# One square a chunk, later sums, far tiles between near ones, later scan masks: four moves in a hybrid encoder step

## The chip, the cores and the metric

The kernel runs on one core of one Trainium2 chip. The metric is the device time of one execution in microseconds: the median of several runs. A second source is one profiled execution, from which the views of the profile (timelines, waits, stretches of the span) come.

## The reference

One layer of a streaming encoder is computed for two groups of tokens that share the weights: 256 tokens of a prompt and 32 of a running stream, 288 columns in all. The model width is 2048.

```python
xn   = rmsnorm(x, norm_mix_pre)
proj = xn @ w_in            # u_pool (1024) | z (2048) | xBC (2560) | dt (32)
pool = pool_mixer(u_pool)   # trailing means over windows 2, 4, 8, 16
y    = ssd_scan(conv_silu(xBC), dt, A, B, C, D, h0)    # 32 heads, state 128
ssd  = grouped_rmsnorm(y * silu(z))
x    = x + rmsnorm(concat(pool, ssd) @ w_out, norm_mix_post)
h    = rmsnorm(x, norm_ffn_pre)
up   = causal_dwconv(h @ w_up, width=3)                # 2 * 5632 columns
x    = x + rmsnorm((silu(gate) * value) @ w_down, norm_ffn_post)
```

The outputs are x for both groups and the new histories and states of the pooling, the convolutions and the scan. All inputs and outputs are 32-bit floats.

## The kernel before

**Tiles and products.** Activations lie transposed: 16 tiles of 128 features by 288 tokens. Every large product is made from three matmuls in a faster 32-bit format: each weight is split into a high part (`whi`, a copy on ACT, L152) and a low part (`wlo`, raw weight less high part, on DVE, L153), each activation too (`xn`, `hn` and others), and `mm3` (L166) adds high by high, high by low and low by high. So for each block of weights (1024 elements a partition) a DMA from SP brings the raw block, ACT splits it, DVE makes the low part, and PE runs 24 matmuls of 288 columns on it. The high parts and the low parts have a fixed number of buffers each, so a split can begin only when PE is done with an older one.

**Order.** A scheduler orders the instructions of each engine by priorities and by a model of their times. Each engine takes its queue strictly in that order, so an instruction that waits holds all behind it. Three things bind the scheduler: `pin` (also `keep_in_program_order`) keeps the written order among pinned instructions, `issue_after` puts one instruction behind another, and `high_priority` draws a part ahead.

**The start (L353 to L397).** The first 768 columns of the input projection are worked off in 11 chunks of the 16 feature tiles (`CHUNKS`; chunks 6 to 10 hold two tiles each). `prepare(i)` makes chunk i's operands one chunk ahead of the products: `xn` high on ACT (L318), the weight's high part on ACT (L330), `xn` low (L321) and the weight's low part (L334) on DVE. Beside it run the squares of the input for the first norm: `squares(q)` squares two tiles on ACT (L353) into `sq`, which has one buffer, and adds them to `sq2` on DVE (L354). The table `SQUARES` says in which chunk's preparation which squares stand. In chunk 9, after 24 products, two matmuls `prs` (L391) sum the squares over the features; ACT takes the root (L394) and DVE the reciprocal (L395), `rstd`, by which every result of the projection is scaled later. The products of a chunk run on PE at L397.

**The scan's masks.** The projection goes on in groups of columns: groups of `xs` (input of the scan, after a convolution with tanh, L459), then groups of `z`. For each quad of heads `ssd_first` fetches the decays and makes `ce` (an exponential, L617), `ssd_tokens` fetches the tokens, and `ssd_masks` makes the mask `m`: 12 Relus (L653), an exponential (L656) and a product on DVE (L658). `run_masks` calls it; `XS_RATE` and `Z_RATE` say after which group how many quads are made. `ssd_products` (L678 to L684) uses the masks on PE.

**Between mixer and FFN (L1097 to L1127).** `x1[s]`, the 16 result tiles of the output projection (tiles `mg`), are each multiplied by the second norm's factor `rm` on DVE (L1119). Then the layer's input is added: for the near tiles (s below `NEAR`, 8) it lies in SBUF and DVE adds it (L1121); for the far tiles GpSimd starts a DMA that adds it from HBM (L1123, 144 KB). `hn_of(t)` then makes the FFN's operand: `hn` high on ACT (L1100), low on DVE (L1101), the square on ACT (L1108, `sq` with two buffers), and the sum of squares on DVE (L1115). The matmuls of the up projection that read `hn` and the weight splits of that projection run at the same time on PE, ACT and DVE.

Of the kernel before, what the change touches and what calls it, by code (L numbers as in the profile page):

```python
# [1 line left out]

# [8 lines left out]
AF = mybir.ActivationFunctionType  # L11
# [17 lines left out]
KD = D_MODEL // P  # L29
# [7 lines left out]
MW = 416  # L37
EVAC = 100
SUMS_AFTER = 2
XS_RATE = (0, 0, 1, 0, 1, 0, 0, 1)  # L40
Z_RATE = (1, 0, 1, 1, 1, 1, 0, 0)
PAIR_XS = (7,)
PAIR_Z = (1, 4, 6)
# [2 lines left out]
CHUNKS = ((0, 1), (1, 1), (2, 1), (3, 1), (4, 1), (5, 1), (6, 2), (8, 2), (10, 2), (12, 2), (14, 2))  # L46
# [8 lines left out]
TURN_AT = 13  # L55
FC_GAP = 48
NEAR = 8
W_GAP = 48
W_ROOM = 64
TURNED_FIRST = (4, 5)  # L60
# [9 lines left out]
def body(  # L70
# [23 lines left out]
    act, dve, pool, pe, sp = nc.scalar, nc.vector, nc.gpsimd, nc.tensor, nc.sync  # L94
# [210 lines left out]
    def prepare(i):  # L305
# [4 lines left out]
        w_ = xin.tile([P, 2 * n * NB + W_ROOM], F32R, tag="w", bufs=3, name="w")  # L310
        hi, lo = (w_[:, c : c + n * NB].rearrange("p (k c) -> p k c", k=n) for c in (0, n * NB + W_GAP))
        w = (hi, lo)
# [34 lines left out]
    def squares(q):  # L347

        src = xg[:, KD + 2 * NT * q : KD + 2 * NT * (q + 1)]
        if q == 0:  # L350
            return pin(act.activation(sq2, src, AF.Square))
        o = xin.tile([P, 2 * NT], F32, tag="sq", bufs=1, name="sq")
        pin(act.activation(o, src, AF.Square))  # L353
        pin(dve.tensor_tensor(sq2, sq2, o, op=ALU.add))  # L354

    SQUARES = {4: (0,), 5: (1,), 6: (2,), 7: (3, 4), 8: (5,), 9: (6,), 10: (7,)}
    early = ExitStack()
    early.enter_context(tc.high_priority(offset=2000))
    ahead_w = [prepare(0)]
    for i, (kb, n) in enumerate(CHUNKS):  # L360
        if i + 1 < len(CHUNKS):
            ahead_w.append(prepare(i + 1))
            for q in SQUARES.get(i + 1, ()):
                squares(q)
        if i == 5:
            first_load(10)
            pin(act.activation(ones_r, ones, AF.Copy))
            pin(dve.memset(ebuf[0][:, 0:1], 0.0))
            for e in ebuf + ubuf:
                pin(pool.memset(e, 0.0))  # L370
        if i == 6:
            pin(dve.tensor_tensor(
                w_dt, w_dt, g_mix_pre.unsqueeze(2).broadcast_to([P, KD, HEADS]), op=ALU.mult
            ))
        if i == len(CHUNKS) - 2:
            pin(dve.tensor_tensor(sq2[:, :NT], sq2[:, :NT], sq2[:, NT:], op=ALU.add))
            sq_r = xin.tile([P, 2 * NT], F32R, tag="sq", bufs=1, name="sq_r")
            pin(dve.tensor_copy(sq_r[:, :NT], sq2[:, :NT]))
            pin(dve.tensor_tensor(sq_r[:, NT:], sq2[:, :NT], sq_r[:, :NT].bitcast(F32), op=ALU.subtract))
        w = ahead_w.pop(0)  # L380
        products = [
            (r, m, k, x) for m in (2, 3, 4, 5, 0, 1) for k in range(n)
            for r, x in (((0, 0), (1, 0), (0, 1)) if i in TURNED_FIRST else ((0, 0), (0, 1), (1, 0)))
        ]
        if i == 0:
            products.sort(key=lambda q: ((q[1] + 4) % 6 // 2, q[0], q[3]))
        for q, (r, m, k, x) in enumerate(products):
            if i == len(CHUNKS) - 2 and q == 24:
                p_ = aux([P, NT], "prs")
                for c in (slice(0, NT), slice(NT, 2 * NT)):  # L390
                    pin(pe.matmul(p_, ones_r, sq_r[:, c], start=c.start == 0, stop=c.start > 0))  # L391
                rstd = const.tile([P, NT], F32, tag="spread", bufs=3, name="rstd")
                last_split[:] = [
                    pin(act.activation(rstd, p_, AF.Sqrt, bias=eps_t, scale=1.0 / D_MODEL)),  # L394
                    pin(dve.reciprocal(rstd, rstd)),  # L395
                ]
            pin(pe.matmul(  # L397
                first[m], w[r][:, k, m * P : (m + 1) * P], xn[kb + k][:, x, :],
                start=kb + k + r + x == 0, stop=kb + k == KD - 1 and r == 1,
            ))  # L400

    for k in range(KD):
        c = slice(HEADS * (k % 4), HEADS * (k % 4 + 1))
# [33 lines left out]
    def conv_in(i, p_):  # L437
# [6 lines left out]
        pool.tensor_copy(e[:, 259:262], hist_c[:, :, i])  # L444
        return e

    def conv_out(i, e, out):

        pool.tensor_copy(
            sc_stage[:, :, :, i], e[:, 256:326].rearrange("p (s c) -> p s c", c=35)[:, :, 0:3]  # L450
        )
        c = mp.tile([P, 291], F32, tag="conv", bufs=2, name="conv")
        act.activation(c, e[:, 0:291], AF.Identity, bias=cb_[:, i : i + 1], scale=cw[:, 0, i : i + 1])
        for r in range(1, 4):
            dve.scalar_tensor_tensor(
                c, e[:, r : r + 291], cw[:, r, i : i + 1], c, op0=ALU.mult, op1=ALU.add
            )
        th = mp.tile([P, 291], F32, tag="tanh", bufs=2, name="tanh")
        act.activation(th, c, AF.Tanh)  # L459
        dve.scalar_tensor_tensor(out[:, :NP_], th[:, :NP_], 1.0, c[:, :NP_], op0=ALU.add, op1=ALU.mult)  # L460
        dve.scalar_tensor_tensor(out[:, NP_:], th[:, 259:], 1.0, c[:, 259:], op0=ALU.add, op1=ALU.mult)

# [35 lines left out]
    with tc.high_priority(offset=EVAC):  # L498
        for i, v in enumerate(v4):
            c = slice(HEADS * i, HEADS * (i + 1))  # L500
# [109 lines left out]
    def ssd_first(q):  # L610

        gb = mp.tile([P, 4, MW], F32, tag="gb", bufs=2, name="gb")
        pool.dma_start(out=gb, in_=g_d[4 * q : 4 * q + 4, :].unsqueeze(0).broadcast_to([P, 4, MW]))
        h0t = mp.tile([P, 2, P], F32, tag="h0t", bufs=2, name="h0t")
        sp.dma_start(out=h0t.rearrange("p i c -> p (i c)"), in_=state_nq[:, 2 * P * q : 2 * P * (q + 1)])
        ce = mp.tile([P, 4, NS], F32, tag="ce", bufs=2, name="ce")
        act.activation(ce, gb[:, :, 384:], AF.Exp)  # L617
        cs = bc[2 + q // 4][:, NP_:]
        dve.tensor_tensor(ce, ce, cs.unsqueeze(1).broadcast_to([P, 4, NS]), op=ALU.mult)
        ready.append((gb, h0t, ce))  # L620
# [3 lines left out]
    exps = []  # L624
# [7 lines left out]
    def ssd_masks(q):  # L632


        gi = q // 4
        if not q:
            ssd_first(0)
        gb, h0t, ce = ready[q]
        xw = tokens.pop(q)
        w = tok[:, :, 1, 4 * q : 4 * q + 4].unsqueeze(3).broadcast_to([P, 3, 4, 64])  # L640
        o = xw.rearrange("p b (r q) -> p b r q", r=4)
        with ExitStack() as order:
            if masked:
                order.enter_context(tc.issue_after(masked[-1].ins))
            dve.tensor_tensor(o, o, w, op=ALU.mult)
        m = mp.tile([P, 4, MW], F32, tag="m", bufs=2, name="m")
        for j in range(4):
            for b, (lo_, hi_) in enumerate(((0, 256), (256, 384), (384, MW))):
                h = 4 * q + j
                with ExitStack() as order:  # L650
                    if exps:
                        order.enter_context(tc.issue_after(exps[-1].ins))
                    act.activation(  # L653
                        m[:, j, lo_:hi_], gb[:, j, lo_:hi_], AF.Relu, bias=tok[:, b, 0, h : h + 1], scale=-1.0
                    )
        exps.append(act.activation(m, m, AF.Exp, scale=-1.0))  # L656
        masked.append(
            dve.tensor_tensor(m, m, cbt[:, gi : gi + 1, :].broadcast_to([P, 4, MW]), op=ALU.mult)  # L658
        )

        if q % 2 == 0:
            ssd_first(q + 1)
        return xw, m, h0t, ce
# [155 lines left out]
    for i in range(1, NX // 2):  # L819
        if XS_RATE[i]:  # L820
            ssd_tokens(quads[0])
# [3 lines left out]
        if i in PAIR_XS:  # L825
            run_pair()
        run_masks(XS_RATE[i])
    for i in range(NX // 2):
# [90 lines left out]

    xT = op_.tile([P, NEAR, NT], F32, name="xT2")  # L920
    x1 = []
# [45 lines left out]
    for gi in range(2):  # L967
        c = slice(gi * P, (gi + 1) * P)
# [96 lines left out]
    for grp in ((0, 1), (2,), (3,), (4,), (5,), (6, 7)):  # L1065
# [13 lines left out]
        if grp[0] == 0:  # L1079
            sp.dma_start(out=xT.rearrange("p k n -> p (k n)"), in_=x_g[:, KD : KD + NEAR * NT])  # L1080
            sp.dma_start(out=new_sconv, in_=sc_stage.rearrange("p s r t -> p (s r t)"))
# [33 lines left out]
            pin(dve.tensor_tensor(xsum, xsum, squares.pop(t - 1), op=ALU.add))  # L1115

    todo = list(range(KD))
    for s in range(KD):
        pin(dve.tensor_tensor(x1[s], x1[s], rm, op=ALU.mult))  # L1119
        if s < NEAR:  # L1120
            pin(dve.tensor_tensor(x1[s], x1[s], xT[:, s, :], op=ALU.add))  # L1121
        else:
            pin(pool.dma_start(out=x1[s], in_=x_g[:, KD + NT * s : KD + NT * (s + 1)], accum_op=ALU.add))  # L1123
        while todo and todo[0] + (1 if todo[0] < NEAR else NEAR) <= s:
            hn_of(todo.pop(0))
    while todo:
        hn_of(todo.pop(0))  # L1127
# [94 lines left out]
    for q in range(4):  # L1222
        for b in range(2):
            t = apool.tile([P, 512], F32, tag="a", name="xr")
# [94 lines left out]
    for n_, part_ in enumerate(parts):  # L1319
        for i, t in enumerate((A, B)):  # L1320
            for k, hi, lo in part_:
                c, end = slice(i * P, (i + 1) * P), k == HALF - 1
# [140 lines left out]
```

## Time and profile before

| | us |
|---|---|
| median of 3 runs | 1305.62 (1305.27 to 1305.78) |
| profiled execution, whole | 1306.34 |
| its span | 1304.6 |
| PE busy | 1296.9 (99%), 10043 instructions |
| DVE busy | 897.0 (69%) |
| ACT busy | 671.6 (51%) |
| GpSimd (POOL) busy | 251.7 (19%) |
| granted clock of PE | 1.00 of full speed |

A row of a timeline gives the start (us from the span's start), the time to the end of the last, the engine, the line, the operation, the tiles written and read, and how many of a kind stand behind one another; in brackets is the idle time before it and what ended that. A matmul's time includes its way through the array, so PE's pace is read from the distance of two starts. PEld is PE's loading of the stationary operand.

### The profile page before, as it was taken

To read this page: it belongs to the slowest core of one execution; us is meant where nothing else is said; L and a number is where in the kernel's file an instruction comes from. 1 tells how busy PE (TensorE), PEld (TensorE's weight loads), DVE (VectorE), ACT (ScalarE), POOL (GpSimd) and SP (SyncE) were. 2 spreads that over 40 slices of the span, in tenths; PEclk is the share of its full clock that TensorE was granted. 3 is DMA by queue.
4 is the path that set the end of the run, shared out by engine and by line. 5 is a ranking of instruction groups with operands and counts; after the bars stand their busy time and mean duration, and the time that the engine had idled before them with its cause. 6 is when DMAs were issued, how large, how long until landed. Compare 5 with 4: busy or idle time off the path is not lost.

```text
span 1304.6 us, 25289 instructions
## 1 busy us (share of the span) xinstructions
PE 1296.9 (99%) x10043; PEld 1286.6 (99%) x10043; DVE 897.0 (69%) x1531; ACT 671.6 (51%) x1013; POOL 251.7 (19%) x399
## 2 busy tenths in 40 slices
PE   9999999999999999999999999999999999999998
PEld 9999999999999999999999999999999999999997
DVE  7999987989655588867766744336666666664454
ACT  7557676646544567554544433334444454444442
POOL 2343231222222231211211100001111111201110
PEclk9999999999999999999999999999999999999999
DMA  8668877445767478766545455455545555466663
GB/s 329 204 211 274 250 242 232 137 166 169 242 213 229 140 198 259 210 185 202 172 162 166 160 170 175 157 175 182 174 162 166 175 175 165 163 233 191 209 182 113
DMA packets 110326, 251.75 MB, mean 193 GB/s; under 512 B 64768, under 2 KB 73888, under 8 KB 87936
## 3 DMA queue, kind: packets, MB, share of 16 engines
q1 hardware_dynamic: 103856, 233.36, 55.7%
q0 software_dynamic: 5824, 16.13, 4.3%
q8 instruction: 78, 1.28, 0.4%
q10 hardware_dynamic: 528, 0.66, 0.2%
q14 instruction: 40, 0.33, 0.1%
HBM read 237.11 MB, written 13.00 MB: 192 GB/s over the span
## 4 chain that ended last, share of the span: by engine, by line
PE 96%; DMA 1%; DVE 1%; ACT 1%; issue 0%; SPq 0%; ACTq 0%
PE acc L166 91%; PE acc_x L166 1%; DMA raw<-in_w_first 1%; PE py L678 1%; PE acc L1324 0%; DVE w L334 0%; PE acc L1325 0%; DMA xg<-in_x_g 0%; PE acc_t L1347 0%; DVE sq L354 0%; PE py L680 0%; PE acc_x L397 0%; PE acc L397 0%; DVE xn L321 0%; PE pst L1036 0%
## 5 line engine op out<-in xcount | busy, mean ns | idle before, releaser
L153 DVE TENSOR_TENSOR wlo<-raw,whi 128x1024 fp32r<-128x1024 f32 (+1 forms) x396 | 472.7, 1196 | 297.1 <-ACT whi L152 296.1
L152 ACT ACTIVATE whi<-raw 128x1024 fp32r<-128x1024 f32 (+1 forms) x396 | 408.0, 1033 | 471.1 <-PE acc L166 381.3
L166 PE MATMUL acc<-hn,whi 128*128 128x288 f32 x2752 | 539.0, 294 | 0.5 <-ACT hn L1100 0.4
L166 PEld LDWEIGHTS acc<-hn,whi 128*128 128x128 f32 x2752 | 436.3, 188 | 1.5 <-ACT hn L1100 0.8
L166 PE MATMUL acc<-hn,wlo 128*128 128x288 f32 x1376 | 399.6, 291 | 0.0
L166 PEld LDWEIGHTS acc<-hn,wlo 128*128 128x128 f32 x1376 | 259.0, 188 | 0.0
L166 PE MATMUL acc<-fa,whi 128*128 128x288 f32 x1320 | 257.5, 293 | 0.0
L166 PE MATMUL acc<-xn,whi 128*128 128x288 f32 x1216 | 238.5, 294 | 0.0
L166 PEld LDWEIGHTS acc<-fa,whi 128*128 128x128 f32 x1320 | 208.9, 188 | 0.0
L166 PEld LDWEIGHTS acc<-xn,whi 128*128 128x128 f32 x1216 | 192.9, 188 | 0.6 <-issue 0.5
L166 PE MATMUL acc<-fa,wlo 128*128 128x288 f32 x660 | 192.1, 291 | 0.0
L166 PE MATMUL acc<-xn,wlo 128*128 128x288 f32 x608 | 177.4, 292 | 0.0
L166 PEld LDWEIGHTS acc<-fa,wlo 128*128 128x128 f32 x660 | 124.3, 188 | 0.0
L1150 POOL COPY fc_stage<-ebuf 128x4 f32<-128x4 f32 x88 | 26.9, 306 | 472.8 <-DVE ebuf L1149 451.4
L166 PEld LDWEIGHTS acc<-xn,wlo 128*128 128x128 f32 x608 | 114.5, 188 | 0.0
L166 PE MATMUL acc<-mixs,whi 128*128 128x288 f32 x512 | 100.2, 293 | 0.0
L1145 POOL COPY ebuf<-cols 128x2 f32<-128x2 f32 x88 | 71.7, 816 | 111.1 <-DVE fc L1156 91.8
L1156 DVE SCALAR_TENSOR_TENSOR fc<-ebuf,cols,fc 128x290 f32<-128x290 f32 x176 | 90.5, 518 | 3.5 <-ACT fc L1154 0.8
L1154 ACT ACTIVATE fc<-ebuf,cols 128x290 f32<-128x290 f32 x88 | 54.4, 623 | 72.4 <-DVE ebuf L1149 72.4
L166 PEld LDWEIGHTS acc<-mixs,whi 128*128 128x128 f32 x512 | 81.1, 188 | 0.0
L166 PE MATMUL acc<-mixs,wlo 128*128 128x288 f32 x256 | 74.6, 291 | 0.0
L166 PE MATMUL acc<-mixp,whi 128*128 128x288 f32 x256 | 50.1, 293 | 0.0
(323 smaller groups left out, 1245.3 us busy)
## 6 DMA issues: line engine op xcount, KB each, us to landing
raw<-in_w_up SPq DMA_DIRECT2D x80, 1024.0 KB, 5.1
raw<-in_w_in SPq DMA_DIRECT2D x38, 1024.0 KB, 5.3
raw<-in_w_down SPq DMA_DIRECT2D x32, 1024.0 KB, 5.0
raw<-in_w_out SPq DMA_DIRECT2D x22, 1024.0 KB, 5.2
raw<-in_w_down SPq DMA_DIRECT2D x16, 768.0 KB, 4.4
raw<-in_w_up SPq DMA_DIRECT2D x14, 512.0 KB, 4.6
gb<-g_d POOLq DMA_DIRECT2D x8, 832.0 KB, 6.4
raw<-in_w_first SPq DMA_DIRECT2D x5, 768.0 KB, 13.0
```

Of the source, the lines that this page charges most:

```text
L152: act.activation(hi, raw[:, k : k + n, :], AF.Copy)
L153: dve.tensor_tensor(lo, raw[:, k : k + n, :], hi.bitcast(F32), op=ALU.subtract)
L166: ins = pe.matmul(out, w, a[:, x, :], start=start and n == 0, stop=stop and n == 2)
L678: ins = pe.matmul(y[c, 0:256], xw[:, 0, f_], m[:, h, 0:256], start=True, stop=False)
L1145: pool.tensor_copy(e[:, 258:260], hist_f[:, :, i])
L1150: pool.tensor_copy(fc_stage[:, :, :, i], e[:, 256:324].rearrange("p (s c) -> p s c", c=34)[:, :, 0:2])
L1154: act.activation(c, e[:, 0:290], AF.Identity, bias=col["f_b"][:, i : i + 1], scale=f_w[:, 0, i : i + 1])
L1156: dve.scalar_tensor_tensor(c, e[:, r_ : r_ + 290], f_w[:, r_, i : i + 1], c, op0=ALU.mult, op1=ALU.add)
```

## The change

Four things are moved; no instruction is added or taken away.

1. **Squares.** The table `SQUARES` gives chunk 4 two squares and each of chunks 5 to 10 one; before, chunk 7 had two. Squares 1, 2 and 3 come a chunk earlier.
2. **Sums.** The two `prs` matmuls stand ahead of chunk 10's first product, where they stood after the first 24 of chunk 9's 36: 12 products later. ACT's root and DVE's reciprocal follow them.
3. **Far and near tiles.** The loop over `x1` runs in the order 0, 1, 2, 3, 8, 4, 9, 5, 10, 6, 11, 7, 12, 13, 14, 15. `hn_of` is called in the loop only for tiles 0 to 6, each behind the product of the next near tile; for the others it is called after the loop.
4. **Masks.** `XS_RATE` puts the first three calls of `ssd_tokens` and `ssd_masks` after groups 5, 6 and 7 of `xs`; before they stood after groups 2, 4 and 7. The first `ce` and the Relus of the first mask are put behind the latest tanh of the convolution that has been written by then.

```diff
-XS_RATE = (0, 0, 1, 0, 1, 0, 0, 1)
+XS_RATE = (0, 0, 0, 0, 0, 1, 1, 1)
...
+FAR_AT = 4
...
-    SQUARES = {4: (0,), 5: (1,), 6: (2,), 7: (3, 4), 8: (5,), 9: (6,), 10: (7,)}
+    SQUARES = {4: (0, 1), 5: (2,), 6: (3,), 7: (4,), 8: (5,), 9: (6,), 10: (7,)}
...
-            if i == len(CHUNKS) - 2 and q == 24:
+            if i == len(CHUNKS) - 1 and q == 0:
                 p_ = aux([P, NT], "prs")
...
-        act.activation(th, c, AF.Tanh)
+        tanhs.append(act.activation(th, c, AF.Tanh))
...
-        act.activation(ce, gb[:, :, 384:], AF.Exp)
+        with ExitStack() as order:
+            if not q:
+                order.enter_context(tc.issue_after(tanhs[-1].ins))
+            act.activation(ce, gb[:, :, 384:], AF.Exp)
...
-                    if exps:
-                        order.enter_context(tc.issue_after(exps[-1].ins))
+                    order.enter_context(tc.issue_after((exps or tanhs)[-1].ins))
...
-    for s in range(KD):
+    turns = list(range(FAR_AT))
+    for near, far in zip_longest(range(FAR_AT, NEAR), range(NEAR, KD)):
+        turns.extend(t for t in (far, near) if t is not None)
+    for s in turns:
...
-        while todo and todo[0] + (1 if todo[0] < NEAR else NEAR) <= s:
+        while todo and todo[0] < s < NEAR:
             hn_of(todo.pop(0))
```

The line numbers after the change are 2 higher from the start on, 4 to 6 higher in the scan and 6 to 9 higher in the loop over `x1`.

**The start, on ACT.** `w_383` (before) and `w_386` (after) are the weight splits of chunk 7, `w_435` that of chunk 8; `xn_436` and `xn_437` are chunk 8's activations. On ACT before:

```order
L330 ACTIVATE w_383<-raw_117 128x1536
L353 ACTIVATE sq_392<-xg_95 128x576
L353 ACTIVATE sq_395<-xg_95 128x576
L318 ACTIVATE xn_436<-xg_95 128x288
L318 ACTIVATE xn_437<-xg_95 128x288
L330 ACTIVATE w_435<-raw_119 128x1536
L353 ACTIVATE sq_444<-xg_95 128x576
```

The same place on ACT after the change:

```order
L332 ACTIVATE w_386<-raw_117 128x1536
L355 ACTIVATE sq_395<-xg_95 128x576
L320 ACTIVATE xn_436<-xg_95 128x288
L320 ACTIVATE xn_437<-xg_95 128x288
L332 ACTIVATE w_435<-raw_119 128x1536
L355 ACTIVATE sq_444<-xg_95 128x576
```

Chunk 8's activations and its weight now stand behind one square, where they stood behind two. The square that is gone here stands in chunk 4's preparation, with its add on DVE.

**The second mask, on ACT.** `m_1633` (before) and `m_1949` (after) are the mask of head quad 1, and the row with 128x1664 is its exponential. On ACT before:

```order
L152 ACTIVATE whi_1814<-raw_1808 128x1024
L152 ACTIVATE whi_1868<-raw_1866 128x1024
L656 ACTIVATE m_1633<-m_1633 128x1664
L453 ACTIVATE conv_1791<-ebuf1_168,pah_641 128x291
L152 ACTIVATE whi_1872<-raw_1866 128x1024
L152 ACTIVATE whi_1971<-raw_1969 128x1024
L459 ACTIVATE tanh_1779<-conv_1774 128x291
L152 ACTIVATE whi_1975<-raw_1969 128x1024
```

The same place on ACT after the change:

```order
L154 ACTIVATE whi_2033<-raw_2027 128x1024
L659 ACTIVATE m_1949<-gb_1780,tok_852 128x32
L457 ACTIVATE conv_2093<-ebuf0_167,pah_641 128x291
L154 ACTIVATE whi_2205<-raw_2203 128x1024
L463 ACTIVATE tanh_1938<-conv_1933 128x291
L154 ACTIVATE whi_2209<-raw_2203 128x1024
L662 ACTIVATE m_1949<-m_1949 128x1664
L154 ACTIVATE whi_2263<-raw_2261 128x1024
```

The exponential stood behind the split `whi_1868`; now it stands behind `whi_2209`, seven splits later.

**The far tiles, on ACT.** The operands `hn_6036` and `hn_6050` belong to tile 7 (before and after), `hn_6056` to tile 8, and so on in steps of one to `hn_6098`, tile 15; `whi_6341`, `whi_6369`, `whi_6397` and `whi_6425` are splits of the second weight block of the up projection. On ACT before:

```order
L1100 ACTIVATE hn_6036<-mg_5050,cols_125 128x288
L1108 ACTIVATE sq_6039<-mg_5050 128x288
L1100 ACTIVATE hn_6056<-mg_5227,cols_125 128x288
L1108 ACTIVATE sq_6059<-mg_5227 128x288
L152 ACTIVATE whi_6341<-raw_6333 128x1024
L1100 ACTIVATE hn_6062<-mg_5244,cols_125 128x288
L152 ACTIVATE whi_6369<-raw_6335 128x1024
L1108 ACTIVATE sq_6065<-mg_5244 128x288
L1100 ACTIVATE hn_6068<-mg_5452,cols_125 128x288
L152 ACTIVATE whi_6397<-raw_6337 128x1024
L1100 ACTIVATE hn_6074<-mg_5469,cols_125 128x288
L152 ACTIVATE whi_6425<-raw_6339 128x512
```

The same place on ACT after the change:

```order
L1106 ACTIVATE hn_6068<-mg_5452,cols_125 128x288
L1106 ACTIVATE hn_6074<-mg_5469,cols_125 128x288
L1114 ACTIVATE sq_6053<-mg_5050 128x288
L1106 ACTIVATE hn_6080<-mg_5828,cols_125 128x288
L1106 ACTIVATE hn_6086<-mg_5845,cols_125 128x288
L1114 ACTIVATE sq_6059<-mg_5227 128x288
L1114 ACTIVATE sq_6065<-mg_5244 128x288
L1114 ACTIVATE sq_6071<-mg_5452 128x288
L1106 ACTIVATE hn_6092<-mg_5894,cols_125 128x288
L154 ACTIVATE whi_6341<-raw_6333 128x1024
L1114 ACTIVATE sq_6077<-mg_5469 128x288
L154 ACTIVATE whi_6369<-raw_6335 128x1024
```

The first of these splits stood behind `hn` of tile 8 and its square; now `hn` of tiles 9 to 14 and the squares of tiles 9 and 10 stand ahead of it too, and one more square ahead of the second split. On DVE the products of tiles 8 to 11 by `rm` have moved between those of tiles 4 to 7, and those of tiles 12 to 15 stand behind two of the low splits of the first block instead of behind all four.

More of the change, by code (lines that the diff above doesn't have):

```diff
@@ L1 @@
 from contextlib import ExitStack
+from itertools import zip_longest
 import concourse.bass as bass
@@ L445, in conv_in @@
         return e
+    tanhs = []
     def conv_out(i, e, out):
```

## The prediction

> **What bounds the kernel now.** I read the page first (busy times, the chain of waits), then what the matrix engine waited for, then the timelines of each engine at the places that the change touches.
>
> ```profile
> span 1304.6 us, 25289 instructions
> PE 1296.9 (99%) x10043; PEld 1286.6 (99%) x10043; DVE 897.0 (69%) x1531; ACT 671.6 (51%) x1013; POOL 251.7 (19%) x399
> PE 96%; DMA 1%; DVE 1%; ACT 1%; issue 0%; SPq 0%; ACTq 0%
> PEld acc L397 <- DVE w L334: 0.6, 2, 0.5
> PEld acc L166 <- ACT whi L152: 0.4, 1, 0.4
> PEld prs L391 <- DVE sq_r L379: 0.3, 1, 0.3
> 47.50:108.00 60.50, 60.50 (x467) 60.30 (x464) 59.90 (x141) 33.02 (x48) 27.84 (x32) 1.00 0.66 202
> 108.00:300.00 192.00, 192.00 (x1611) 188.83 (x1611) 169.23 (x316) 129.54 (x241) 48.89 (x58) 1.00 0.67 213
> 479.08:501.97 22.89, 22.75 (x171) 22.39 (x169) 20.82 (x39) 15.24 (x27) 7.03 (x8) 1.00 0.87 217
> ```
>
> PE is busy 99% of the span and holds 96% of the chain; the change neither adds nor removes a matmul, so it can only fill or open PE's gaps. The rows from PEld (columns: total, times, longest) list nearly all that can be gained: half a microsecond at a chunk weight, 0.3 at the sums, 0.4 at a weight split. The last three rows are stretches of the span (us from its start); after their length come the busy time of PE, PEld, DVE, ACT and POOL, then the granted clock, the DMA share and GB/s.
>
> **The change part by part.** The profiled run took 1306.34 us, the span plus 1.74; it lies 0.72 over the median of the three runs, 1305.62. I sum against the span and add the sum to the median.
>
> *Squares and sums (0 to 47 us).*
>
> ```profile
> 20.36 1.35 PE L397 MATMUL acc<-xn,w 128*128 128x288 f32 x9
> 28.18 1.72 PE L397 MATMUL acc_x<-xn,w 128*128 128x288 f32 x12
> 29.74 0.42 PE L397 MATMUL acc<-xn,w 128*128 128x288 f32 x2
> 30.41 0.80 PE L397 MATMUL acc<-xn,w 128*128 128x288 f32 x4 [0.25 <-DVE w L334]
> 37.31 1.10 PE L397 MATMUL acc<-xn,w 128*128 128x288 f32 x7
> 38.34 0.89 PE L391 MATMUL prs<-sq_r,ones_r 128*128 128x288 f32 x2
> 39.07 0.56 PE L397 MATMUL acc_x<-xn,w 128*128 128x288 f32 x3
> 13.76 0.67 ACT L351 ACTIVATE sq<-xg 128x576 f32<-128x576 f32 x1
> 14.33 0.52 ACT L318 ACTIVATE xn<-xg 128x288 fp32r<-128x288 f32 x1
> 21.66 1.49 ACT L330 ACTIVATE w<-raw 128x1536 fp32r<-128x1536 f32 x1 [1.64 <-DMA raw<-in_w_first]
> 25.65 0.68 ACT L353 ACTIVATE sq<-xg 128x576 f32<-128x576 f32 x1 [1.93 <-DVE sq L354]
> 18.42 1.76 DVE L334 TENSOR_TENSOR w<-raw,w 128x1536 fp32r<-128x1536 f32 x1 [0.31 <-ACT w L330]
> 28.60 1.76 DVE L334 TENSOR_TENSOR w<-raw,w 128x1536 fp32r<-128x1536 f32 x1
> 38.32 0.46 DVE L379 TENSOR_TENSOR sq_r<-sq,sq_r 128x288 fp32r<-128x288 f32 x1
> ```
>
> From 28.18 to 29.74 PE starts twelve products, so its pace is 0.130 us. After the two at 29.74 the next was due at 30.00 and started at 30.41; its four took 0.80 where four at that pace take 0.68, a ramp of 0.11. Chunk 8 thus loses 0.52. The cause is on ACT: the second square of chunk 7 (25.65) waited 1.93 us for the one `sq` buffer, held the chunk-8 split behind it, and put the low part of that weight at 28.60 on DVE. ACT had gone idle at 23.72 (25.65 − 1.93). With one square in chunk 7 it goes on to chunk 8's operands there, 2.5 us sooner (the wait and the square); DVE has 0.9 of its own work still in front of the low part, which so comes about 1.6 sooner, 27.0 to 28.8, ahead of the 30.00 at which PE asks: −0.52.
>
> The sums lose as much: from 37.31, seven products and two sums should reach 38.48, but the next product started at 39.07, 0.58 later, since `sq_r` ended at 38.78 (38.32 + 0.46). The work is done about 1.6 us sooner by the same missing wait, and PE now asks at about 39.6, so −0.58. Moving the sums 12 products alone (12 × 0.13 = 1.57) would cover that too. Behind it the root and the reciprocal come 0.9 us later, which delays the evictions that DVE makes with it.
>
> The square goes into chunk 4, where ACT and DVE have little slack: one costs ACT 0.57 us (13.76 to 14.33). ACT's next free wait is that for raw weights before 21.66 (1.64), which absorbs it, but chunk 6's low part (18.42 to 20.18) moves to 20.75, and PE, in chunk 6 from 20.36, asks for it at its third product, 20.62: 0.13 to 0.18 and a ramp, +0.29. The start gives −0.52 − 0.58 + 0.29 = −0.81.
>
> ```profile
> 64.50 1.20 DVE L153 TENSOR_TENSOR wlo<-raw,whi 128x1024 fp32r<-128x1024 f32 x1
> 69.77 0.29 PE L166 MATMUL acc<-xn,wlo 128*128 128x288 f32 x1
> ```
>
> DVE, which the late reciprocal sets back, is full from 47.5 to 108 (59.90 of 60.50), so it cannot catch up there. What hides the 0.9 and PE's own 0.81 is the lead of its low weight splits over PE. The smallest lead in the stretch is that of the split at 64.50: it ended at 65.70, and its first product started at 69.77, 4.07 later. A lead of 4.1 less 1.7 still covers, so I take 0; without that cover it would be up to 1.7.
>
> *Masks (115 to 155 us).*
>
> ```profile
> 128.40 1.89 DVE L658 TENSOR_TENSOR m<-m,cbt 128x1664 f32<-128x1664 f32 x1
> 144.19 1.06 ACT L152 ACTIVATE whi<-raw 128x1024 fp32r<-128x1024 f32 x1 [1.54 <-PE acc L166]
> 147.31 1.06 ACT L152 ACTIVATE whi<-raw 128x1024 fp32r<-128x1024 f32 x1 [1.73 <-PE acc L166]
> 152.24 0.63 PE L678 MATMUL py<-m,xk 128*64 128x256 f32 x4
> ```
>
> The mask of quad 1 (four heads) was ready at 130.29 and is used first at 152.24. Now ACT takes quad 1's exponential right behind the split that stood at 144.19, so at about 145.6 to 147.1; DVE's product (1.89), behind what it has in its queue (a low split of 1.2 at most), then ends near 150.2. PE asks at 152.24 − 0.81 = 151.4. The margin shrinks from 22 us to 1.2. I price it at 0, with 1.9 more if it slips by one split's turn (3.1, from 144.19 to 147.31). A gain is excluded: PE was busy all of 108 to 300 (192.00 of 192.00). The scan's token tile comes 18 small matmuls later on PE, at no cost of its own: the same matmuls run.
>
> *Far and near tiles (467 to 502 us).*
>
> ```profile
> L1123 POOL DMA_DIRECT2D mg<-in_x_g x8: 848/1727/2959, 480.4 to 487.6; - x8
>   ACT hn L1100: 6.6, 2
> DMA to landing us min/median/max: 5.4/6.0/8.9
> 471.32 0.45 DVE L1119 TENSOR_TENSOR mg<-mg,rm 128x288 f32<-128x288 f32 x1
> 479.99 2.96 DVE L153 TENSOR_TENSOR wlo<-raw,whi 128x1024 fp32r<-128x1024 f32 x3
> 483.66 2.67 DVE L1119 TENSOR_TENSOR mg<-mg,rm 128x288 f32<-128x288 f32 x7
> 486.17 0.54 ACT L1100 ACTIVATE hn<-mg,cols 128x288 fp32r<-128x288 f32 x1 [4.95 <-DMA mg<-in_x_g]
> 486.61 0.43 ACT L1108 ACTIVATE sq<-mg 128x288 f32<-128x288 f32 x1
> 487.11 1.06 ACT L152 ACTIVATE whi<-raw 128x1024 fp32r<-128x1024 f32 x1
> 490.26 0.70 PE L166 MATMUL acc<-hn,whi 128*128 128x288 f32 x4
> 493.10 0.30 PEld L166 LDWEIGHTS acc<-hn,whi 128*128 128x128 f32 x2 [0.38 <-ACT whi L152]
> ```
>
> Before, ACT waited 6.6 us for two far tiles, yet the stretch from 479.08 lost PE only 22.89 − 168 × 0.13 = 1.05 (168 products start in it; its row also counts three that overlap its edges). Tile 8 is now multiplied at 471.32, where near tile 4 stood, tiles 9 to 11 two microseconds apart behind it, and by 6 us to landing all four are there by 484. But tiles 12 to 15 come only after the near ones. Before, two and a half low splits stood ahead of the far products at 483.66; one and a half of these (1.2 us a whole one) now stand behind them, so tile 12 is multiplied at about 481.8, the others 0.37 apart. With DVE's 0.45, POOL's turn of 0.3 and 5.4 to 6.0 to landing, tile 12 arrives at 488.0 to 488.5, the others by 490. And ACT's queue is new: the splits of the next weight block, of which the first ran at 487.11 between `hn` 8 and 9, now stand behind `hn` 8 to 14 and their squares up to tile 10. So: tile 12 lands at 488.0; `hn` 12 and 13 and two squares bring ACT to 489.6; the third square waits for DVE's add to free its buffer, to 490.1, and takes 0.45; `hn` 14 to 491.0; the first split ends near 491.95. PE asks 84 products after 479.08, at 490.0: 1.95 and a ramp of 0.1. The second split, behind one more square, ends at 493.25 and is asked for four products later, about 492.5: 0.75 and 0.1. Together 2.9, in place of 1.05: +1.85. By the shortest landing (5.4) it is 0.6 less; by the longest (8.9), 2.9 more.
>
> The Trainium skill, "DMA: Bandwidth & Descriptors", section "Anatomy of one DMA — SWDGE (gpsimd) path", gives a GpSimd DMA 2.0 us plus its bytes over 436 GB/s; by that, tile 12 would be there at an estimated 484.7, no tile would hold ACT, and the sum would be that of the first rival. The trace disagrees: 5.4 us at least for these eight.
>
> Sum: −0.81 + 1.85 = +1.04, a span of about 1305.6, a profiled run of 1307.4, and 1306.7 on the scale of the median. What can be told from no change here is about 0.2%, 2.6 us.
>
> **The rivals.** *First: the far tiles no longer hold ACT.* If the transfers, spread out instead of in a burst of seven, land in about 3 us, the first split is ready by its slot and all of the 1.05 goes: −0.81 − 1.05 = −1.86, 1303.8. For it: 4.95 of ACT's 6.6 us of waiting was for tile 8, which starts nine microseconds sooner. Against it: the shortest landing of the eight is 5.4, and the last four go off together still. Chance 0.20.
>
> *Second, slower: the last four far tiles land late.* At 8.9 us tile 12 is there at 491.3 instead of 488.0 to 488.4, and the stall grows by 2.9: 1309.6. It decides from a landing of about 7 us on. For it: 8.9 was seen in the burst before. Against it: this burst has four transfers, not seven. Chance 0.10.
>
> *Third, slower: quad 1's mask is late.* If one more weight split (3.1 us between their turns) comes ahead of the exponential, PE waits 3.1 − 1.2 = 1.9 at 151 us: 1308.6. It decides from a delay of 1.2 us on, one DVE low split. For it: DVE is busy 169.23 of 192 there. Against it: nothing ahead of it is late in the trace of before. Chance 0.12.
>
> *Fourth: the squares don't help,* because the wait at 25.65 only moves to chunk 8's raw weights, as chunk 7's split had to wait 1.64 for its own. Then the start gives about 0 and the kernel takes 1305.62 + 1.85 = 1307.5. Against it: the wait would have to last 1.9. Chance 0.06.
>
> **How the numbers follow.** The forecast, 1306.7, has 0.52. The range takes the first rival's end with 0.2 to spare and the second's: 1303.6 to 1309.6. Faster by over 0.2% (below 1303.0) needs more than the first rival's 1.86: 0.04. Slower by over 0.2% (above 1308.2) are the second and third rival and the forecast's upper edge, two terms late at once: 0.10 + 0.12 × 0.8 + 0.02 = 0.22. The rest, 0.74, is no difference.
>
> **What would show it.** In the changed profile: no 0.25 wait at chunk 8's weight, no wait of the sums, a new wait of about 0.2 near 20.6 for the low part of chunk 6; the weight splits of the second block of the up projection starting near 491 on ACT, and PE waiting for them 1.5 to 2 us at about 490 and half a microsecond at 492.5; no PE wait at 150 to 153. I am wrong if ACT's wait for `in_x_g` at tile 12 is missing, if PE waits at L678's new line, or if chunk 8 still waits.

## The result and the profile after

The changed kernel takes 1310.37 us (median of 6 executions, 1309.51 to 1310.85) against 1305.3 for the kernel before in the same session (6 executions, 1304.76 to 1305.78): 1.0039 times as long, 95% interval 1.0027 to 1.005. It is 5.1 us slower, where 1306.7 was forecast with a range up to 1309.6. The profiled execution took 1310.17 us.

The page of the changed kernel, its span, busy times and chain:

```profile
span 1308.5 us, 25281 instructions
PE 1298.4 (99%) x10043; PEld 1288.9 (99%) x10043; DVE 898.2 (69%) x1531; ACT 671.5 (51%) x1013; POOL 246.6 (19%) x399
PE 96%; issue 2%; DMA 1%; POOL 1%; ACT 0%; DVE 0%; POOLq 0%; ACTq 0%
```

PE does the same 10043 matmuls and is still busy 99%, so the page alone hides the loss. The waits of PE and PEld in the changed kernel (total, times, longest; PEld's row is the same wait seen from the weight load) show some 3 us of it:

```profile
PE acc L168 <- ACT whi L154: 3.0, 2, 2.5
PEld acc L168 <- ACT whi L154: 3.5, 2, 2.7
```

The waits for chunk 8's weight and for the sums, listed before, are gone; the one wait that has clearly grown is this one. Its place is the one that the prediction named. PE's timeline of the changed kernel there:

```profile
489.78 0.29 PE L168 MATMUL acc_x<-hn,wlo 128*128 128x288 f32 x1
492.57 0.79 PE L168 MATMUL acc<-hn,whi 128*128 128x288 f32 x4 [2.50 <-ACT whi L154]
493.85 0.88 PE L168 MATMUL acc<-hn,whi 128*128 128x288 f32 x4 [0.49 <-ACT whi L154]
494.53 0.44 PE L168 MATMUL acc<-hn,wlo 128*128 128x288 f32 x1
494.77 0.68 PE L168 MATMUL acc<-hn,whi 128*128 128x288 f32 x2
495.25 0.44 PE L168 MATMUL acc<-hn,wlo 128*128 128x288 f32 x1
```

The product due at 489.91 starts at 492.57, 2.66 late, and the fifth behind it 0.65 late. But then, with no wait at all, the starts from 494.53 on lie 0.24 apart instead of 0.13 (0.72 for three, 494.53 to 495.25). Stretches of the same trace, and in the last row of the kernel before, with the granted clock in the column ahead of the last two:

```profile
491.00:494.41 3.41, 1.35 (x8) 1.12 (x9) 3.41 (x8) 3.41 (x7) 0.00 (x0) 1.00 0.04 13
494.41:497.82 3.41, 3.41 (x16) 3.41 (x16) 3.41 (x6) 1.95 (x4) 0.00 (x0) 0.50 0.68 193
494.00:498.00 4.00, 4.00 (x19) 4.00 (x20) 4.00 (x7) 2.36 (x5) 0.00 (x0) 0.57 0.63 177
489.00:500.00 11.00, 8.01 (x48) 7.55 (x47) 9.06 (x17) 8.12 (x15) 0.00 (x0) 0.84 0.53 140
489.00:500.00 11.00, 10.86 (x81) 10.50 (x80) 9.95 (x19) 9.87 (x19) 1.58 (x2) 1.00 0.97 242
```

Behind the stall the clock was half, 0.50, for 3.41 us (second row); over the four microseconds from 494 that is 0.57 on average. In the 11 us from 489 PE started 48 matmuls where it had started 81 (last two rows): 33 × 0.13 = 4.3 us. That is nearly the whole loss.

The rest is in a place where nothing waits. Stretches of 40 us behind the start, before and after:

```profile
60.00:100.00 40.00, 40.00 (x310) 40.00 (x309) 39.63 (x91) 20.48 (x29) 17.49 (x15) 1.00 0.69 206
60.00:100.00 40.00, 40.00 (x302) 40.00 (x302) 38.59 (x89) 19.85 (x29) 11.89 (x15) 1.00 0.65 191
```

PE is busy 40.00 of 40.00 at clock 1.00 in both, and yet starts 302 matmuls where it started 310. The pace is 0.1333 us a product instead of 0.1300. By PE's starts, the 408 products behind the first weight block (from about 51 to 104 us) take 54.40 us in place of 53.04: +1.36.

The start itself gained. PE and DVE in the changed kernel, at the sums and at chunk 8:

```profile
38.54 0.43 PE L393 MATMUL prs<-sq_r,ones_r 128*128 128x288 f32 x2
38.81 1.49 PE L399 MATMUL acc<-xn,w 128*128 128x288 f32 x10
25.87 1.75 DVE L336 TENSOR_TENSOR w<-raw,w 128x1536 fp32r<-128x1536 f32 x1
35.63 0.46 DVE L381 TENSOR_TENSOR sq_r<-sq,sq_r 128x288 fp32r<-128x288 f32 x1
```

The sums run at pace (0.27 for two), `sq_r` is ready at 36.09, 2.4 us ahead, and chunk 8's low part ends at 27.62, before its products. At 45 us the changed trace leads the one before by 1.73 us; 0.77 of this is there by the 60th instruction on PE, when the changed squares do not yet count.

In sum, in this pair of traces: −1.73 in the start, +1.4 from 48 to 114, +4.3 from 489 to 500, together +4.0; the spans differ by 3.9.

### The profile page after: what moved, and what is told of

Its sections match the earlier page's. It is cut to its first block, busy times and chain, and to the rows that moved or that the text cites. A ratio compares the mean times of both kernels' runs of the same rounds, so it can differ in the third digit from the quotient of the medians.

```text
span 1308.5 us, 25281 instructions
## 1 busy us (share of the span) xinstructions
PE 1298.4 (99%) x10043; PEld 1288.9 (99%) x10043; DVE 898.2 (69%) x1531; ACT 671.5 (51%) x1013; POOL 246.6 (19%) x399
## 4 chain that ended last, share of the span: by engine, by line
PE 96%; issue 2%; DMA 1%; POOL 1%; ACT 0%; DVE 0%; POOLq 0%; ACTq 0%
PE acc L168 89%; PE acc L399 2%; PE acc_x L399 1%; PE acc_x L168 1%; PE py L684 1%; DMA mg<-in_x_g 1%; PE acc L1333 0%; PE acc L1334 0%; PE acc_t L1356 0%; POOL mg L1132 0%; PE py L686 0%; DMA xg<-in_x_g 0%; POOL ho L1061 0%; PE acc L406 0%; PE py_s L690 0%
```

## The experiments

Each time stands beside the kernel before in the same session (its median 1305.58, 1305.28, 1305.18 or 1305.42 us). A ratio has its 95% interval. "The 408 products" are those just named.

### The far tiles alone, and the change without them

The kernel before with part 3, and the changed kernel with part 3 undone:

```diff
-    for s in range(KD):
+    for s in turns:
...
-        while todo and todo[0] + (1 if todo[0] < NEAR else NEAR) <= s:
+        while todo and todo[0] < s < NEAR:
```

> The kernel before with the far and near order of the changed kernel alone (part 3). Theory A, the order of ACT's queue behind the far tiles makes the whole loss: PE waits about 2.5 us at 490 and 0.5 at 493 for the weight splits, the granted clock drops for 3 to 4 us behind it, and the time is 4.4 us over before (1309.7 at a before of 1305.3). Rival B, the loss needs the rest of the change as well (earlier squares, later masks): then this kernel stays within 1.5 us of before.

Measured: 1309.74, ratio 1.0032 (1.0021 to 1.0042). The far tiles' order alone makes 4.2 of the 5.1 us.

> The changed kernel with part 3 undone (squares, sums and masks stay changed). Theory A: 0.3 us under before (1305.0), since the start gains 1.7 and the stretch from 45 to 108 us gives 1.4 back at a product pace of 0.1333 us instead of 0.130. Rival B: still 3 us or more over before.

Measured: 1306.12 beside 1305.58, ratio 1.0006 (0.9997 to 1.0015). Rival B falls in both. The three other parts together gain nothing, where theory A had 0.3 under before. PE in the far tiles' order alone, and a stretch behind:

```profile
492.54 0.80 PE L168 MATMUL acc<-hn,whi 128*128 128x288 f32 x4 [2.16 <-ACT whi L154]
493.83 0.80 PE L168 MATMUL acc<-hn,whi 128*128 128x288 f32 x4 [0.48 <-ACT whi L154]
494.00:498.00 4.00, 4.00 (x31) 4.00 (x32) 4.00 (x7) 2.61 (x6) 0.00 (x0) 1.00 0.66 175
```

The stalls are nearly those of the changed kernel (0.34 less in the first), but in this one execution the clock stayed at 1.00, and it was 1308.97. Over the eight executions of this kernel the mean clock went from 0.999 to 0.996, and the time with it, from 1307.41 to 1311.43. So the clock's drop seems to belong to most executions, not to all. The mean is a blunt sign of it: in every trace the clock is also half in the last 0.1 to 3.4 us of the span, and that alone moves the mean by up to 0.001. The kernel before has 0.999 or 1.0 in all its executions.

### The splits ahead of the last far tiles

The changed kernel, with `hn` of tiles 12 to 15 made in the up projection, behind the splits of the second weight block:

```diff
+            if late_hn and kb == 12:
+                late_hn.pop(0)(split_ins[-1])
...
-    while todo:
+    while todo[0] < 12:
         hn_of(todo.pop(0))
```

> The changed kernel (all four parts) with one thing more: hn of tiles 12 to 15 and their squares are placed behind the four weight splits of the second block in ACT's queue (their squares in free buffers, summed apart and added at the end). Theory A, what stands ahead of the splits in ACT's queue is the whole loss: PE no longer waits at 490 and 493 for these splits, the clock stays 1.00 there, and the time is 3.7 to 4.7 us under the changed kernel, 1305.5 to 1306.5 at a before of 1305.6. Rival B, the far transfers themselves or DVE's later low splits hold PE: PE still loses 2 us or more between 489 and 502.

Measured: 1306.56 beside 1305.28, ratio 1.0011 (1.0003 to 1.002): 1.3 over before where the changed kernel lies 5.1 over, so 3.8 of the 5.1 are gone, as theory A said, though the time lies 0.4 over its figures at this before. The waits on PE in its trace:

```profile
PE acc L171 <- ACT whi L157: 0.4, 1, 0.4
490.10 0.70 PE L171 MATMUL acc<-hn,whi 128*128 128x288 f32 x4
491.23 0.66 PE L171 MATMUL acc<-hn,whi 128*128 128x288 f32 x3 [0.43 <-ACT whi L157]
```

With the far products and transfers left as in the changed kernel, taking `hn` 12 to 15 from in front of the splits removes the stall at 490, and the clock doesn't drop in this trace. One short wait is left (0.59 with its pipeline). Rival B falls: the loss was the order of ACT's queue. The edit moves DVE's work on these four tiles (their low parts and sums) behind the splits too and gives their squares free buffers, so it doesn't part these from ACT's order; that PE waited for ACT's splits is read from the trace of the changed kernel.

> The kernel before with the new table of squares, the far tiles between near ones, and the splits ahead of hn 12 to 15 as in the run before; sums and masks as before. Theory A: the start gains 0.4 to 1.2, the pace stays 0.130 from 45 to 108 us, and the 0.9 us that the kernel before loses from 479 to 502 goes too: 1 to 2 us under before, 1303.6 to 1304.6. Rival: a new wait for hn 12 to 15 or their sum takes that back, time within 0.4 of before.

Its edit is the same on the kernel before with parts 1 and 3. Measured: 1305.2 beside 1305.28, ratio 1.0 (0.9991 to 1.0009). The expected gain isn't there. The same 0.59 wait stands at 490.9, and the 1.05 us that the prediction counted as lost in the kernel before is not a fixed loss: in the trace of the change without part 3, which has the old order there, PE waits for nothing from 469 to 505.

### A far tile sooner

The changed kernel with `FAR_AT = 3` in place of 4, which leaves three far tiles in the last burst.

> The changed kernel with the far tiles begun one near tile sooner (FAR_AT 3): tile 12 is multiplied ahead of tile 7, and hn of tile 14 instead of a burst of four stands ahead of the first split. Theory A, the stall is set by when the last far tile ahead of the split lands, and the clock drops only when the stall is long enough: PE waits about 1.8 us at 490 instead of 2.5 and 0.3 to 0.7 at 493, no drop of the clock in the trace, 1.5 to 2.5 us under the changed kernel (1308.0 to 1309.0 at a before of 1305.4). Rival B, one set loss for the interleaving: as the changed kernel, 1310 and more.

Measured: 1309.23 beside 1305.18, ratio 1.003 (1.0019 to 1.004), 0.8 under the changed kernel in the same session (1310.02).

```profile
493.00 0.79 PE L168 MATMUL acc<-hn,whi 128*128 128x288 f32 x4 [1.36 <-ACT whi L154]
494.57 0.40 PE L168 MATMUL acc<-hn,wlo 128*128 128x288 f32 x1 [0.79 <-DVE wlo L155]
```

The first stall is 1.52 (expected 1.8), the clock held in the trace, and its mean is 0.999 in seven of the eight executions (0.998 in the slowest). But the second stall grew, now for the low part on DVE: 0.95, and a third, 0.32, came at 481. The first stall was cut as expected, but theory A left out the second: 0.8 was saved where it had 1.5 to 2.5. How much of the 0.8 is the clock that held isn't shown.

> The changed kernel once more, for the spread of its executions beside the others. Theory A, two equal stalls in ACT's queue and a clock that drops in most executions but not in all: median 1309.5 to 1310.5; executions with a mean clock of 0.999 lie 1 to 2 us under those with 0.997 to 0.998. Rival: the clock plays no part, and the time doesn't go with it.

Measured: five executions, 1309.69 to 1311.64, median 1310.02, ratio 1.004 (1.0027 to 1.0053). The two at a mean clock of 0.997 took 1311.31 and 1311.64, the two at 0.998 took 1309.69 and 1310.02, the one at 0.999 took 1309.81. The median is as expected; but the one at 0.999 is not 1 to 2 us under those at 0.998, so the time goes with the mean clock only in part, and five executions are few. PE in the trace of this second execution, and the stretch in which its clock was half:

```profile
492.68 0.79 PE L168 MATMUL acc<-hn,whi 128*128 128x288 f32 x4 [2.06 <-ACT whi L154]
493.42:496.83 3.41, 2.92 (x13) 2.87 (x13) 3.41 (x5) 3.05 (x6) 0.00 (x0) 0.50 0.46 147
```

The first stall is 2.23 here, the second 0.65 as before, and the clock was half for 3.41 us. In the far tiles' order alone stalls of 2.32 and 0.65 left the clock at 1.00. So the length of the stall alone does not decide whether the clock drops.

### Squares, sums and the pace behind them

> The kernel before with the new table of squares alone (part 1). Theory A1, the sums' wait goes with the squares alone and the slow pace from 45 to 108 us comes from where the two sums' products stand in PE's stream: the start gains 1.2 to 1.7, the pace stays 0.130, time 1.2 to 1.7 under before (1303.6 to 1304.1). Theory A2, the slow pace comes from the missing stall in chunk 8: pace 0.1333 from 45 to 108, time within 0.5 of before.

The kernel before with the new table `SQUARES` alone. Measured: 1305.17 beside 1305.58, ratio 0.9997 (0.9988 to 1.0006); the pace is 0.130, so A1 is right on the pace and wrong on the gain: 0.4, which can't be told from nothing.

The kernel before with the sums 12 products later, nothing else:

```diff
-            if i == len(CHUNKS) - 2 and q == 24:
+            if i == len(CHUNKS) - 1 and q == 0:
```

> The kernel before with the two sums' products 12 products later (part 2 alone). Theory A, where the two products stand sets PE's pace behind them: 0.1333 us from 45 to 108, +1.4, less 0.6 for the sums' wait: 0.8 over before (1306.4). Rival C, pace follows the stall in chunk 8 that stays here: 0.130, time 0.6 under before (1305.0).

Measured: 1307.79 beside 1305.28, ratio 1.0019 (1.0011 to 1.0028). Two stretches of 40 us, of squares alone and of sums alone:

```profile
60.00:100.00 40.00, 40.00 (x309) 40.00 (x309) 39.56 (x94) 19.93 (x30) 17.61 (x15) 1.00 0.67 197
60.00:100.00 40.00, 40.00 (x302) 40.00 (x302) 38.58 (x89) 19.95 (x30) 12.15 (x15) 1.00 0.66 195
174.49 0.40 PE L166 MATMUL acc<-xn,wlo 128*128 128x288 f32 x1 [0.73 <-DVE wlo L153]
```

The place of the two sums' products sets the pace (302 against 309). Of the 1.7 us over the expectation 1.0 is the last row (with its ramp), a wait for a low split at 173 us, which the changed kernel doesn't have. Chunk 8 lost nothing in this trace, with the old squares: that stall isn't in every execution.

The order of one block's three products sets the pace too. In the blocks that the table `TURNED` names, `mm3`'s second and third product change places. Part 3 undone and the turned block of the first column group taken away; then the same taken away from the kernel before:

```diff
-    1: (0,), 5: (3,),
+    5: (3,),
```

> The changed kernel without part 3, and with the first weight block of the first column group in the usual order of its three products instead of the turned one (all the same matmuls; only their order in that block). Theory A, the pace is a state of PE's product stream that a turned block flips: the stretch from 45 to 108 us goes back to 0.130 us a product, time 1.4 under the kernel without part 3 (1303.6). Rival C, the pace there is set by what shares the memory with PE (DVE, DMA at their later times): it stays 0.1333, time 1305.0.

Measured: 1305.1 beside 1305.58, ratio 0.9999 (0.999 to 1.0008); 1.0 under the same kernel with the turned block, and 1.5 over the expected time.

> The kernel before with the first weight block of the first column group in the usual order of its three products (TURNED without group 1; the same matmuls). Theory A, PE's pace behind the start is one of two states, and the turned block and the place of the two sums each flip it: the 408 products from 48 to 101 us take 54.40 us instead of 53.04, time 1.2 to 1.5 over before (1306.6 to 1306.9). Rival C, the usual order is simply the faster one there, as it was in the changed kernel: 53.04, time as before (1305.4).

Measured: 1305.94 beside 1305.18, ratio 1.0006 (0.9997 to 1.0015): 0.8 over before where 1.2 to 1.5 was expected, and by the interval not clear of nothing. The pace is clear. The same 40 us, of the two in this order:

```profile
60.00:100.00 40.00, 40.00 (x310) 40.00 (x309) 39.47 (x91) 20.85 (x30) 13.29 (x15) 1.00 0.66 195
60.00:100.00 40.00, 40.00 (x302) 40.00 (x301) 38.81 (x90) 19.94 (x29) 18.45 (x15) 1.00 0.66 196
```

The same edit makes the changed kernel's stretch fast and that of the kernel before slow: 53.04 and 54.40 for the 408 products, to the hundredth the two figures that all earlier runs had. So rival C falls: it is neither the load on memory nor one order that is better in itself. It is a state with two paces, which the sums' place and the turned block both switch.

The rule of the switch was tried next. 

> The changed kernel without the far tiles' order (as in e2), and with the sums 12 products later still, after chunk 10's first 12. Alternation: the state flips back, 408 products in 53.04 us, 0.5 to 1.0 us under before (1304.4 to 1304.9). One fast place only: 54.40, time 0.5 over before as e2.

Measured: 1306.72 beside 1305.42, ratio 1.001 (1.0001 to 1.0019). The 408 products took 53.06, as the alternation says; but the time is 1.3 over before: there is a wait of 0.65 at the first column group, and in the stretch from 114 to 150 us, which had been fast in every run above, PE goes at the slow pace. Before, and here:

```profile
114.00:150.00 36.00, 36.00 (x279) 36.00 (x279) 33.51 (x63) 24.27 (x41) 9.55 (x16) 1.00 0.84 248
114.00:150.00 36.00, 36.00 (x273) 35.84 (x273) 33.40 (x66) 26.22 (x50) 14.99 (x14) 1.00 0.84 251
```

> The kernel before with the sums 12 products sooner (after chunk 9's first 12). Alternation, and one fast place only: 54.40 us for the 408 products, time 1.4 over before or more, since the sums also wait longer. If it stays 53.04, the place counts only behind a certain point.

Measured, in one execution: 1309.2, and 53.32 for the 408 products: not the slow pace (310 matmuls from 60 to 100 us, as before). But its stream was disturbed ahead of that, by a stall of 1.7 us ahead of the first sum (the 1.52 below and its pipeline), of 0.4 at the second, and by the clock behind them:

```profile
37.24 0.89 PE L391 MATMUL prs<-sq_r,ones_r 128*128 128x288 f32 x2 [1.52 <-DVE sq_r L378]
40.00:43.00 3.00, 3.00 (x17) 3.00 (x17) 3.00 (x4) 2.46 (x3) 0.00 (x0) 0.64 0.00 0
```

> The kernel before with the second weight block of the first column group turned as well as the first. Alternation: the second turned block flips the state again, the products from 51 to 101 us run at the slow pace, 54.3 to 54.4 for the 408. A turned block that sets the state rather than flips it: 53.0 to 53.2.

Measured, in one execution: 1305.64, 53.09 for the 408 products. A second turned block leaves the fast pace: it does not flip it. With the run before it this speaks against the plain alternation. What sets the state is not settled.

A stall can switch it as well. The changed kernel's two traces differ in the start: in the second PE waited for chunk 6's low part, in the first it hardly did. PE in the second, then 14 us of the first and of the second; then 20 us of the kernel before, and of the changed kernel without the far tiles' order and with the sums after chunk 10's first 12, which had a stall of 0.36 at 202 us:

```profile
20.14 3.20 PE L399 MATMUL acc<-xn,w 128*128 128x288 f32 x22 [0.41 <-DVE w L336]
22.00:36.00 14.00, 14.00 (x110) 14.00 (x109) 13.83 (x18) 10.81 (x17) 10.53 (x12) 1.00 0.98 351
22.00:36.00 14.00, 14.00 (x108) 14.00 (x107) 13.82 (x18) 10.85 (x17) 10.87 (x13) 1.00 1.00 360
200.00:220.00 20.00, 20.00 (x156) 20.00 (x155) 14.26 (x20) 8.68 (x12) 4.79 (x4) 1.00 0.67 227
200.00:220.00 20.00, 19.91 (x150) 19.68 (x149) 15.44 (x20) 8.49 (x12) 6.16 (x5) 1.00 0.60 204
```

By PE's starts the pace is 0.1300 in the second and fourth row and 0.1333 in the third and, behind the stall, in the last. The first two come from the same kernel, so the order of the instructions alone does not set the state. Not every stall switches it (with the masks alone a stall of 0.36 at the sums was followed by 0.1300), and the 408 products took 54.40 in both traces of the changed kernel.

### The masks, and a try for the better of both

> The kernel before with the later masks alone (part 4). Both theories: no wait of PE at the masks (L684 and around, 148 to 155 us), time within 0.4 of before. A rival by which the quad 1 mask is late: PE waits 1 us or more at 150 us.

Measured: 1305.26 beside 1305.28, ratio 1.0001 (0.9992 to 1.001). The masks cost nothing, as forecast. In the changed kernel, quad 1's product and the first use:

```profile
148.62 1.85 DVE L664 TENSOR_TENSOR m<-m,cbt 128x1664 f32<-128x1664 f32 x1
151.91 0.63 PE L684 MATMUL py<-m,xk 128*64 128x256 f32 x4
```

It ends at 150.47, 1.44 ahead of PE; 1.2 was forecast.

> The kernel before with another table of squares (chunks 4 to 9 one each, two in chunk 10, so that chunk 4 keeps one), the sums 24 products later than before (after chunk 10's first 12), and TURNED without group 1; far tiles and masks as before. Theory A: no wait of PE at chunk 6 or 8 nor at the sums, pace 0.130 from 48 to 101 us: 0.5 to 1.2 us under before (1304.2 to 1304.9). Rival: the two squares in chunk 10 make the sums late, PE waits there 0.5 us or more, and time is as before or over it.

The edit, beside the turned block taken away as above:

```diff
-    SQUARES = {4: (0,), 5: (1,), 6: (2,), 7: (3, 4), 8: (5,), 9: (6,), 10: (7,)}
+    SQUARES = {4: (0,), 5: (1,), 6: (2,), 7: (3,), 8: (4,), 9: (5,), 10: (6, 7)}
...
-            if i == len(CHUNKS) - 2 and q == 24:
+            if i == len(CHUNKS) - 1 and q == 12:
```

Measured: 1307.25 beside 1305.18, ratio 1.0013 (1.0004 to 1.0022). Chunk 6, chunk 8 and the sums don't wait, as expected; but the 408 products took 54.40, the stretch from 114 to 150 us was slow too (273 matmuls), and the first column group waited 0.65. Theory A's pace failed here, and none of the kernels run is clearly faster than the kernel before.

## Why the prediction was wrong, step by step

**Which step failed.** Two steps. The far tiles' term had the right place and the right sign, but it was mis-sized: +1.85 was forecast, and alone part 3 costs 4.2. And the premise that the change "can only fill or open PE's gaps" was false: the pace changed with no gap at all, and the three other parts, forecast at −0.81, gave +0.5. These two places make 2.35 and 1.35 of the 4.0 between forecast and result. Of the 1.35 the pace is 1.0, by the medians of the change without part 3 with and without the turned block (1306.12 and 1305.1); the rest is a smaller gain in the start. What is left, 0.3, these medians don't resolve.

**Far tiles.** ACT's timeline in the changed kernel, and in the last row the time that its far transfers took:

```profile
486.66 0.54 ACT L1106 ACTIVATE hn<-mg,cols 128x288 fp32r<-128x288 f32 x1 [3.52 <-DMA mg<-in_x_g]
489.31 0.54 ACT L1106 ACTIVATE hn<-mg,cols 128x288 fp32r<-128x288 f32 x1 [2.11 <-DMA mg<-in_x_g]
490.70 0.44 ACT L1114 ACTIVATE sq<-mg 128x288 f32<-128x288 f32 x1 [0.19 <-DVE msum L1121]
491.48 1.04 ACT L154 ACTIVATE whi<-raw 128x1024 fp32r<-128x1024 f32 x1
492.76 1.04 ACT L154 ACTIVATE whi<-raw 128x1024 fp32r<-128x1024 f32 x1
DMA to landing us min/median/max: 3.3/5.0/7.6
```

The mechanism stands in it: ACT waits for tiles 12 and 13, makes their `hn`, two squares, a square that waits for its buffer, `hn` 14, and then the splits. Three sizes were off. *First*, the stall: 2.66 and 0.65 and two ramps of 0.1, 3.5 together, for 2.9. Tile 12 came sooner than forecast (486.66 for 488.0); tile 13, priced at the same moment, came 2.65 behind it, so that the first split ended at 492.52 for 491.95. *Second*, what the stall replaces: 1.05 was taken from one trace as a fixed loss of the kernel before, and traces with the old order show less or none of it. *Third*, missing altogether: the clock. In this trace thirteen products 0.24 apart, 0.11 each over the pace, are 1.4 us. I read the clock of the kernel before (1.00 throughout) and never asked what a stall of 2 us does to it; the kernel before has no such stall behind the start to ask it of.

The Trainium skill, "TensorE: Matmul & The Clock Gate", section "What's actually happening", says that the clock halves after an idle window of some 3.4 us and that these windows run free of the kernel. The traces agree with the half clock, with a stay of 3.41 us in it, and with a drop that comes by chance: a first stall of 2.23 us met it in one execution, one of 2.32 did not in another. They differ in one thing: PE was not idle for a window. It was busy for 1.35 of the 3.41 us ahead of the drop, and with the sums 12 products sooner stalls of 1.7 and 0.4 us were enough.

**The start.** −0.81 was forecast. By medians it gave 0.4 (squares alone, within the interval of none). The waits at chunk 8 and at the sums went as said. The new wait at chunk 6, priced at 0.29, was 0.10 in the first trace of the changed kernel and 0.68 in the second. And chunk 8's stall (−0.52) comes only in some executions of the kernel before: with the old squares it is in the trace of before and in that of the far tiles alone, and not in those of the sums alone, the sums sooner, the masks alone, and the kernel before without the turned block. Without it the forecast's own terms leave −0.29, near what was measured. One trace can't tell a habit from a mishap. Moving the sums added a loss.

**The pace.** No step spoke of it: the same matmuls run, so I put it at nothing. It is +1.36 in the changed kernel, and the reason that parts 1, 2 and 4 end 0.5 over before rather than under it. The trace of before had shown the slow pace too, for some 6 us behind chunk 8's stall (0.1333 by PE's starts, 46 products from 31.05 to 37.19), and I did not look at what that was.

**The masks and the rivals.** The masks were right, and so was the 4 us lead of the low splits: PE waits for none of them from 48 to 108 us in the changed kernel. The second rival, a later landing, gave 1309.6 for a larger stall. The stall did grow, but by 0.6 and not by 2.9, so that rival's price was met by another mechanism. The first rival fell: ACT waited 3.52 and 2.11 for far tiles. So did the fourth: chunk 8's low part was there in time. Its outcome, next to no gain in the start, came near all the same, by other ways.

## What to carry to other kernels

A wait in one engine's queue is priced by the last transfer ahead of it, one at a time, and not by the first of a burst. Where a stall of a microsecond or two is forecast on a busy matrix engine, add what the clock may do behind it, and weigh it as a chance: in one trace here it added 1.4 us to stalls of 3.5, and with nearly the same stalls it did not come in another. And where all waits are gone and the time hasn't moved, count starts in a fixed stretch: a busy share of 100% has two paces here.

## What was not expected of the hardware

- PE's pace has two states at the same clock and the same products: 0.1300 and 0.1333 us (408 products in 53.04 or 54.40 us). Where two extra products stand, and the order of three products in one block of 24, switch it for the 50 us behind; in two traces a stall was followed by the slow pace where the fast one stood without it. What decides is open.
- Behind a stall of 2.66 us and a second of 0.65 the clock was half for 3.41 us (0.24 us a product for 13 products), and so it was with 2.23 in the first; with 2.32 in the first it stayed at 1.00.
- The accumulating transfers of 144 KB landed in 3.3 to 7.6 us in the changed kernel; of the four sent together, the second could be used 2.65 us behind the first (2.5 in the second trace of this kernel, 2.2 in the far tiles alone).
